# Retention norms: the epsilon row is added to one partition of a square on GpSimd, in place of a third product on TensorE

## The chip, the cores and the metric

The kernel runs on one core of one Trainium2 chip. The metric is the time of one execution on the device in microseconds; lower is better. Engines are named as the profile names them: PE is TensorE (matmuls; PEld its weight loads), DVE is VectorE, ACT is ScalarE, POOL is GpSimd and SP is SyncE, which here only issues transfers. An engine works through its own list of instructions in order; a "q" behind its name (SPq, POOLq) is the side that waits and issues.

## What is computed

A trunk of two layers over x of 1024 positions by 1024 features, in float32. Layer 0 mixes by forgetting attention, layer 1 by retention; each is followed by a SwiGLU block, and each block has an RMS norm ahead of it. The change lies in the norm at the end of the retention, over the 512 features of one head:

```python
def retention(h, w_in, w_out):          # 4 heads, 256 key and 512 value features each
    ...
    _, y = lax.scan(step, state0, (qc, kc, vc))
    y = y.transpose(1, 0, 3, 2, 4).reshape(B, S, H, dv)
    mu = jnp.mean(y, axis=-1, keepdims=True)
    var = jnp.mean(jnp.square(y - mu), axis=-1, keepdims=True)
    y = ((y - mu) * lax.rsqrt(var + EPS)).reshape(B, S, H * dv).astype(h.dtype)
    return (jax.nn.silu(g) * y) @ w_out
```

## The kernel before

Activations are kept transposed: features lie on the 128 partitions, positions along the row, in halves of 512 positions. Float32 products are made of three products in a faster format: each operand is split into a high part (ACT, line 105) and the rest (DVE, line 106), and high x high, high x low and low x high are accumulated in one bank of PSUM. So most work of PE comes as triples of matmuls over 512 columns, each triple waiting for a split by ACT and DVE.

The retention's core runs over eight stages: four heads `h`, and for each the two halves `ib` of the positions. They are called (h, ib) here. The loop at the end of the code below makes, for each stage, the weighted sums over the values (`weighted`, lines 1206 to 1208; four banks of PSUM, one for each 128 of the 512 features), puts the scores of the next stage between them (`scores`, lines 1180 to 1182; their splits at lines 105, 106, 1195, 1196), and ends with `finish`. Ahead of a head's first use, `prepare` loads its keys and queries (`load_parts`, line 1109: eight transfers on POOL's queue for the keys, eight for the queries, each 128 x 512) and its values (SP's queue, line 1095).

`finish` is the norm of a stage. For each of the four groups of 128 features ACT copies the bank to SBUF (line 1227) and squares it (line 1232 for the first group, straight into the sum `yacc`; line 1235 for the others), and DVE adds each further square to `yacc` (line 1236). The sum is split into `ah` and `al`, and PE adds up its 128 partitions with a matrix of ones (lines 1241 and 1243, into the bank `sm`). The values were divided by factors that differ from position to position, so epsilon becomes a row of its own, one number for each position. Before the change that row stands, split into high and low part, in two partitions of a tile `ez` whose other partitions are zero, and a third product with the matrix of ones (line 1242) adds it to the sums. ACT and DVE then make the inverse root (lines 1245 to 1249), and DVE scales the four groups (line 1251; for head 0 also by the gate, line 1255).

The epsilon rows are made once, ahead of the stages: a transposed tile of 32 x 128 is scaled and split (lines 1082 and 1083) and written to DRAM (`ed`, line 1086, POOL's queue). Line 1088 sets the whole of `ez` to zero. Each stage loads its 512 numbers of both rows into `ez` (line 1222, POOL's queue). There is one buffer `ez`, so the load for the next stage waits until line 1242 of this stage has read it.

The order of instructions on each engine isn't that of the code: a scheduler sets it by a model of the times (`schedule_with_timeline_sim=True`), and may also move an instruction that the change doesn't touch. POOL's list holds the loads of line 1109, those of line 1222 and, with the change, the additions; each waits in that order.

Of the kernel before, what the change touches and what calls it, by code (L numbers as in the profile page):

```python
# [10 lines left out]
F32 = mybir.dt.float32  # L11
F32R = mybir.dt.float32r
AF = mybir.ActivationFunctionType
ALU = mybir.AluOpType
# [3 lines left out]
P = 128  # L18
S = 1024
D = 1024  # L20
KT = D // P
H = 512
TB = S // P
EPS = 1e-6
FOX_HEADS = 8
RET_HEADS = 4
# [11 lines left out]
def trunk(ctx, tc, nc, d, out):  # L38
    cp = ctx.enter_context(tc.tile_pool(name="cp", bufs=1))
    yp = ctx.enter_context(tc.tile_pool(name="yp", bufs=16))  # L40
    dp = ctx.enter_context(tc.tile_pool(name="dp", bufs=1, space=DRAM))
# [6 lines left out]
    onesr = cp.tile([P, P], F32R, tag="ones", name="ones")  # L48
# [5 lines left out]
    R = cp.tile([P, S], F32, tag="R", name="R")  # L54
# [4 lines left out]
    def nm(s):  # L59
        cnt[0] += 1  # L60
        return f"{s}_{cnt[0]}"
# [10 lines left out]
    def mm_ps():  # L72
        tag, n = (("mm", 3), ("st", 2), ("pv", 2), ("mm", 3), ("st", 2), ("pv", 2), ("mm", 3))[banks[0] % 7]
        banks[0] += 1
        return mp.tile([P, H], F32, tag=tag, name=nm("mm"), bufs=n)

    def yu(s):
        return yp.tile([P, H], F32, tag="y", name=nm(s))

    def yr(s):  # L80
        return yp.tile([P, H], F32R, tag="y", name=nm(s))
# [22 lines left out]
    def split(hi, lo, src):  # L104
        nc.scalar.copy(hi, src)  # L105
        return nc.vector.tensor_tensor(lo, src, hi.bitcast(F32), op=ALU.subtract)  # L106
# [102 lines left out]
    with ExitStack() as fs:  # L209
# [6 lines left out]
        def half(tag, bufs=2):  # L216
            if tag in ("t", "x"):
                return yp.tile([P, H], F32, tag="y", name=nm(tag))
            return fp.tile([P, H], F32, tag=tag, name=nm(tag), bufs={"rec": 1}.get(tag, bufs))
# [4 lines left out]
        for kt in range(KT):  # L224
            xs = []
            for h in range(2):
                t = half("t", 9)
# [215 lines left out]
        for h in range(2):  # L443
            ks.append([fp.tile([P, S], F32R, tag=t, name=nm(t)) for t in ("kh", "kl")])
            for b in range(2):
                tag, n = (("mm", 3), ("mm", 3), ("st", 2), ("st", 2))[2 * h + b]
# [23 lines left out]
        for h in range(FOX_HEADS):  # L470
            if h > 0:
                kk, qq = k1 if h == 1 else k_head(h), q_head(h)
                if h % 2 == 0:
                    vs, _ = v_pair(h // 2, rc)
# [15 lines left out]
        for i, (n, b) in enumerate(TILES):  # L490
            if i < 3:
                mm_u(ops[n, b], wo[n][6:], last_o[:1], b, first=False, last=(i < EVAC))
            else:
                if n == len(wo):
                    wo.append(wtile(d["fox_o"][n][:, :7 * P], 7))
                tag, bufs = TAGS[i]
# [14 lines left out]
    sp = ctx.enter_context(tc.tile_pool(name="sp", bufs=1))  # L511
# [22 lines left out]
    class Combos:  # L534
# [27 lines left out]
        def finish(self):  # L562
            for n in self.rest[0]:
                for j in range(4):
                    self.t[n][j] = bsplit(self.pools[n], self.rest[j][n])
# [370 lines left out]
    for n in range(KT):  # L936
# [5 lines left out]
        for b in range(2):  # L942
            if (n, b) in ops:
                ps = ops[n, b]
            elif n < NPART:
                ps = mp.tile([P, H], F32, tag=("pv", "st")[b], name=nm("mm"), bufs=2)
            else:
                ps = mm_ps()
# [129 lines left out]
    ps = mp.tile([P, H], F32, tag="ms", name=nm("tr"))  # L1078
    n = RET_HEADS * TB
    nc.tensor.transpose(ps[:n, :P], rho.rearrange("p h b -> p (h b)"), ident)  # L1080
    er = [yr("er")[:n, :P] for _ in range(2)]
    nc.scalar.activation(er[0], ps[:n, :P], AF.Copy, scale=512 * EPS)
    nc.vector.scalar_tensor_tensor(er[1], ps[:n, :P], 512 * EPS, er[0].bitcast(F32), op0=ALU.mult, op1=ALU.subtract)
    ed = dp.tile([2, RET_HEADS * S], F32, tag="ed", name="ed")
    for i, t in enumerate(er):
        nc.gpsimd.dma_start(ed[i].rearrange("(n p) -> n p", p=P), t.bitcast(F32))
    ez = sp.tile([P, H], F32R, tag="xo", name="ez", bufs=2)
    nc.scalar.activation(ez, R[:, :H], AF.Copy, scale=0.0)

    mask = sp.tile([P, H], F32, tag="xo", name="mask", bufs=2)  # L1090
    nc.sync.dma_start(mask, d["ret_mask"])
# [127 lines left out]
                nc.tensor.matmul(yps[vt], sl[:, vs], qh, start=False, stop=False)  # L1219

    def finish(h, ib, yps):
        nc.gpsimd.dma_start(ez.bitcast(F32)[:2, :], ed[:, h * S + ib * H:h * S + (ib + 1) * H])
        acc = sp.tile([P, H], F32, tag="sacc", name=nm("yacc"), bufs=2)
        ys = []
        for vt in range(4):
            y = yu("yt")
            cp_ = nc.scalar.copy(y, yps[vt])
            if vt == h == ib == 0:
                with tc.issue_after(cp_.ins):
                    nc.scalar.preload_act_table_set("natural_log_exp_and_others")  # L1230
            if vt == 0:
                nc.scalar.activation(acc, y, AF.Square)
            else:
                sq = yu("sq")
                nc.scalar.activation(sq, y, AF.Square)
                nc.vector.tensor_tensor(acc, acc, sq, op=ALU.add)
            ys.append(y)
        hi, lo = yr("ah"), yr("al")
        split(hi, lo, acc)
        ps = mp.tile([P, H], F32, tag="ms", name=nm("sm"))  # L1240
        nc.tensor.matmul(ps, onesr, hi, start=True, stop=False)
        nc.tensor.matmul(ps, onesr, ez, start=False, stop=False)
        nc.tensor.matmul(ps, onesr, lo, start=False, stop=True)
        q, fb = yu("q"), yu("fb")
        nc.scalar.activation(q, ps, AF.Ln, scale=1.0 / 512)
        nc.scalar.activation(q, q, AF.Exp, scale=-0.5)
        nc.vector.scalar_tensor_tensor(fb, ps, -0.5 / 512, q, op0=ALU.mult, op1=ALU.mult)
        nc.vector.tensor_tensor(fb, fb, q, op=ALU.mult)
        nc.vector.scalar_tensor_tensor(fb, fb, 1.5, q, op0=ALU.add, op1=ALU.mult)
        for vt in range(4):  # L1250
            nc.vector.tensor_tensor(ys[vt], ys[vt], fb, op=ALU.mult)
            if h < 1:
                g = yu("g")
                nc.sync.dma_start(g, gd[4 * h + vt][:, HALF[ib]])
                nc.vector.tensor_tensor(ys[vt], ys[vt], g, op=ALU.mult)
            nc.sync.dma_start(zd[4 * h + vt][:, HALF[ib]], ys[vt])
# [5 lines left out]
    for i, (h, ib) in enumerate(stages):  # L1262
        nxt = stages[i + 1] if i < 7 else None
        if ib == 1 and nxt:
            prepare(h + 1)
        yps = [mm_ps() for _ in range(4)]
        if ib == 1:
            crossed(h, yps)
        an = []
        for dg in range(4):  # L1270
            if nxt:
                an.append(scores(*nxt, dg))
            weighted(h, ib, dg, a[dg], yps)
        a = an
        finish(h, ib, yps)
        if ib == 1 and nxt:
            heads[h + 1][4] = state(h + 1, heads[h + 1][1], heads[h + 1][3])
# [4 lines left out]
    for n in range(KT):  # L1282
        w = wtile2(d["ret_o"][n], 8)
        for h in range(2):
            ps = mm_ps()
            mm_u(ps, w, acts, h)
            y[n][h] = yu("y")
            xo = sp.tile([P, H], F32, tag="sc", name=nm("xo"), bufs=4)
# [98 lines left out]
```

## Time and profile before

| | us |
|---|---|
| median of three runs | 2575.42 |
| lowest and highest of them | 2571.53, 2575.9 |
| the profiled execution | 2571.2 |
| its span, from the first to the last instruction | 2569.4 |

The profile is of one execution. Its rows give times in us from the start of the span; a row of the timeline is the start, the length, the engine, the line, the operation, the tiles that it writes and reads, their shapes and a count. In brackets stands how long the engine had been idle before, and what ended that. Lines are those of the kernel before (L1242 is line 1242). Matmuls overlap, so their lengths are longer than the step from one start to the next. The eight products of line 1242 start between 1631.6 and 1764.3 us.

### The profile page before, as it was taken

To read this page: it belongs to the slowest core of one execution; us is meant where nothing else is said; L and a number is where in the kernel's file an instruction comes from. 1 tells how busy PE (TensorE), PEld (TensorE's weight loads), DVE (VectorE), ACT (ScalarE), POOL (GpSimd) and SP (SyncE) were. 2 spreads that over 40 slices of the span, in tenths; PEclk is the share of its full clock that TensorE was granted. 3 is DMA by queue.
4 is the path that set the end of the run, shared out by engine and by line. 5 is a ranking of instruction groups with operands and counts; after the bars stand their busy time and mean duration, and the time that the engine had idled before them with its cause. 6 is when DMAs were issued, how large, how long until landed. Compare 5 with 4: busy or idle time off the path is not lost.

```text
span 2569.4 us, 35133 instructions
## 1 busy us (share of the span) xinstructions
PE 2546.4 (99%) x12653; PEld 2165.3 (84%) x12653; DVE 1846.1 (72%) x3093; ACT 1250.2 (49%) x2345; POOL 240.5 (9%) x263
## 2 busy tenths in 40 slices
PE   9999999999999999999999999999999999999998
PEld 8889887888888887889898989888888888888888
DVE  6798888976666777886666566786568666668695
ACT  6566656643333455454344445673354333335543
POOL 0143323000000001001111111210000000000200
PEclk9999999999999999999999999999999999999999
DMA  3111142432332344533343335866522223225541
GB/s 131 46 58 58 58 144 83 159 111 99 111 104 96 120 162 159 176 111 118 109 156 127 124 127 174 280 226 219 193 98 86 107 99 111 103 82 192 170 151 66
DMA packets 145903, 327.92 MB, mean 128 GB/s; under 512 B 17552, under 2 KB 30896, under 8 KB 145728
## 3 DMA queue, kind: packets, MB, share of 16 engines
q1 hardware_dynamic: 136368, 297.79, 33.9%
q0 software_dynamic: 8640, 27.34, 3.1%
q8 instruction: 99, 1.62, 0.3%
q14 instruction: 76, 0.62, 0.1%
q10 hardware_dynamic: 720, 0.55, 0.1%
HBM read 225.44 MB, written 100.17 MB: 127 GB/s over the span
## 4 chain that ended last, share of the span: by engine, by line
PE 93%; DVE 3%; issue 2%; DMA 1%; ACT 1%; POOL 0%; POOLq 0%; DVEq 0%; ACTq 0%
PE mm L676 18%; PE mm L677 18%; PE mm L678 18%; PE mm L113 7%; PE mm L114 7%; PE mm L115 7%; PE mm L796 2%; PE mm L794 2%; PE mm L795 2%; PE mm L282 1%; PE mm L281 1%; PE mm L280 1%; PE mm L1207 1%; PE mm L1208 1%; PE mm L1206 1%
## 5 line engine op out<-in xcount | busy, mean ns | idle before, releaser
L677 PE MATMUL mm<-b,wh 128*128 128x512 f32 x2128 | 827.9, 389 | 1.2 <-DVE b L106 1.2
L676 PE MATMUL mm<-b,wh 128*128 128x512 f32 x2128 | 825.7, 390 | 1.5 <-DVE 22_1856_9302 L736 1.1
L678 PE MATMUL mm<-b,wl 128*128 128x512 f32 x2128 | 824.4, 389 | 0.0
L105 ACT CAST wh<-st 128x512 fp32r<-128x512 f32 (+4 forms) x450 | 276.1, 615 | 497.0 <-PE mm L677 318.6
L676 PEld LDWEIGHTS mm<-b,wh 128*128 128x128 f32 x2128 | 399.5, 188 | 85.4 <-DVE 22_1856_9302 L736 1.5
L678 PEld LDWEIGHTS mm<-b,wl 128*128 128x128 f32 x2128 | 399.5, 188 | 83.7 <-DVE wl L106 0.3
L677 PEld LDWEIGHTS mm<-b,wh 128*128 128x128 f32 x2128 | 399.5, 188 | 83.5 <-DVE b L106 1.6
L106 DVE TENSOR_TENSOR wl<-st,wh 128x512 fp32r<-128x512 f32 (+4 forms) x450 | 309.5, 692 | 181.6 <-ACT wh L105 174.0
L105 ACT CAST wh<-s 128x512 fp32r<-128x512 f32 x252 | 156.5, 622 | 295.0 <-PE mm L677 260.7
L113 PE MATMUL mm<-b,wh 128*128 128x512 f32 x736 | 285.8, 392 | 8.9 <-ACT b L133 4.9
L114 PE MATMUL mm<-b,wh 128*128 128x512 f32 x736 | 286.7, 390 | 0.0
L115 PE MATMUL mm<-b,wl 128*128 128x512 f32 x736 | 286.4, 390 | 0.0
L106 DVE TENSOR_TENSOR wl<-s,wh 128x512 fp32r<-128x512 f32 x252 | 179.9, 716 | 102.3 <-ACT wh L105 98.2
L113 PEld LDWEIGHTS mm<-b,wh 128*128 128x128 f32 x736 | 138.3, 188 | 39.2 <-ACT b L133 5.6
L115 PEld LDWEIGHTS mm<-b,wl 128*128 128x128 f32 x736 | 138.5, 188 | 28.4
L114 PEld LDWEIGHTS mm<-b,wh 128*128 128x128 f32 x736 | 138.5, 188 | 27.6
L795 PE MATMUL mm<-wl,b 128*128 128x256 f32 x448 | 126.4, 283 | 0.0
L794 PE MATMUL mm<-wh,b 128*128 128x256 f32 x448 | 126.2, 283 | 0.0
L796 PE MATMUL mm<-wh,b 128*128 128x256 f32 x448 | 125.9, 283 | 0.0
L524 POOL DMA_DIRECT2D b<-ac_B x24 | 13.3, 555 | 1195.7 <-PE mm L677 1192.9
L628 DVE TENSOR_TENSOR s<-st 128x512 f32<-128x512 f32 x84 | 58.2, 693 | 77.0 <-DMA st<-ffn_in 37.8
L105 ACT CAST b<-st 128x512 fp32r<-128x512 f32 (+1 forms) x136 | 77.9, 606 | 58.0 <-DVE st L832 17.9
(564 smaller groups left out, 4141.0 us busy)
## 6 DMA issues: line engine op xcount, KB each, us to landing
st<-ffn_in SPq DMA_DIRECT2D x88, 512.0 KB, 3.6
st<-ffn_out_pairs SPq DMA_DIRECT2D x32, 512.0 KB, 4.3
ac_T<-t SPq DMA_DIRECT2D x48, 256.0 KB, 2.3
xo<-xd SPq DMA_DIRECT2D x32, 256.0 KB, 2.9
ac_B<-t SPq DMA_DIRECT2D x32, 256.0 KB, 2.5
st<-ac_T SPq DMA_DIRECT2D x16, 512.0 KB, 4.7
b<-ac_T POOLq DMA_DIRECT2D x32, 256.0 KB, 5.7
st<-ret_qk SPq DMA_DIRECT2D x16, 512.0 KB, 4.3
```

The source lines that it names most:

```text
L105: nc.scalar.copy(hi, src)
L106: return nc.vector.tensor_tensor(lo, src, hi.bitcast(F32), op=ALU.subtract)
L113: nc.tensor.matmul(ps, wh, xh, start=(first and k == 0), stop=False, skip_group_check=free)
L114: nc.tensor.matmul(ps, wh, xl, start=False, stop=False, skip_group_check=free)
L115: nc.tensor.matmul(ps, wl, xh, start=False, stop=(last and k == n - 1), skip_group_check=free)
L628: nc.vector.tensor_tensor(self.s1, self.a21, self.a22, op=ALU.add)
L676: nc.tensor.matmul(ps, hi[:, js], th, start=first and j == 0, stop=False, skip_group_check=True)
L677: nc.tensor.matmul(ps, hi[:, js], tl, start=False, stop=False, skip_group_check=True)
L678: nc.tensor.matmul(ps, lo[:, js], th, start=False, stop=(j == 3), skip_group_check=True)
L794: nc.tensor.matmul(o, th[:, tk], hi[:, js], start=f, stop=False, skip_group_check=True)
L795: nc.tensor.matmul(o, th[:, tk], lo[:, js], start=False, stop=False, skip_group_check=True)
L796: nc.tensor.matmul(o, tl[:, tk], hi[:, js], start=False, stop=(j == 3), skip_group_check=True)
```

## The change

One row of epsilon, unsplit, replaces the two rows. It is loaded into one partition, and POOL adds it to partition 0 of the square of the second group of features (`vt == 1`), before DVE adds that square to `yacc`. The product of line 1242 is gone, and so are the second half of the split, the second write to DRAM and the zeroing of `ez`.

```diff
-    er = [yr("er")[:n, :P] for _ in range(2)]
-    nc.scalar.activation(er[0], ps[:n, :P], AF.Copy, scale=512 * EPS)
-    nc.vector.scalar_tensor_tensor(er[1], ps[:n, :P], 512 * EPS, er[0].bitcast(F32), op0=ALU.mult, op1=ALU.subtract)
-    ed = dp.tile([2, RET_HEADS * S], F32, tag="ed", name="ed")
-    for i, t in enumerate(er):
-        nc.gpsimd.dma_start(ed[i].rearrange("(n p) -> n p", p=P), t.bitcast(F32))
-    ez = sp.tile([P, H], F32R, tag="xo", name="ez", bufs=2)
-    nc.scalar.activation(ez, R[:, :H], AF.Copy, scale=0.0)
+    er = yu("er")[:n, :P]
+    nc.scalar.activation(er, ps[:n, :P], AF.Copy, scale=512 * EPS)
+    ed = dp.tile([1, RET_HEADS * S], F32, tag="ed", name="ed")
+    nc.gpsimd.dma_start(ed[0].rearrange("(n p) -> n p", p=P), er)
+    ez = sp.tile([P, H], F32, tag="xo", name="ez", bufs=2)[:1, :]
...
     def finish(h, ib, yps):
-        nc.gpsimd.dma_start(ez.bitcast(F32)[:2, :], ed[:, h * S + ib * H:h * S + (ib + 1) * H])
+        nc.gpsimd.dma_start(ez, ed[:, h * S + ib * H:h * S + (ib + 1) * H])
...
                 nc.scalar.activation(sq, y, AF.Square)
+                if vt == 1:
+                    nc.gpsimd.tensor_tensor(sq[:1, :], sq[:1, :], ez, op=ALU.add)
                 nc.vector.tensor_tensor(acc, acc, sq, op=ALU.add)
...
         nc.tensor.matmul(ps, onesr, hi, start=True, stop=False)
-        nc.tensor.matmul(ps, onesr, ez, start=False, stop=False)
         nc.tensor.matmul(ps, onesr, lo, start=False, stop=True)
```

The scheduler's order changes with it, at many places between the eight stages. Lines after the change are three lower than before up to `finish` (line 1106 is the old 1109, 1177 the old 1180), and line 1234 is the new addition.

On POOL, ahead of stage (1, 0), before: the keys and then the queries of head 1 (`kd1`, `qd1`), and after all of them the epsilon load for stage (0, 1).

```order
L1109 DMA b_15773<-kd11h 128x512
L1109 DMA b_15774<-kd11l 128x512
L1109 DMA b_15803<-qd10h 128x512
L1109 DMA b_15804<-qd10l 128x512
L1109 DMA b_15807<-qd11h 128x512
```

The same place after the change:

```order
L1106 DMA b_15769<-kd11h 128x512
L1106 DMA b_15770<-kd11l 128x512
L1234 TENSOR_TENSOR sq_15709<-sq_15709,ez 1x512
L1219 DMA ez<-ed 1x16x32
L1106 DMA b_15799<-qd10h 128x512
L1106 DMA b_15800<-qd10l 128x512
L1106 DMA b_15803<-qd11h 128x512
```

The addition of stage (0, 0) and the next epsilon load now stand between the keys and the queries of head 1. In the same way the addition of (0, 1) stands ahead of head 2's keys, that of (1, 0) ahead of head 3's keys, and that of (1, 1) ahead of head 3's queries.

On PE, at the sum of stage (0, 0), before (`ah`, `al` are the parts of the sum of squares, `ez` the epsilon rows; the products of line 1180 are the first that read head 1's queries, `b_15803`):

```order
L1207 MATMUL mm_15870<-wl_15632,b_15483 128x384
L1241 MATMUL sm_15730<-ah_15726,ones 128x512
L1242 MATMUL sm_15730<-ez,ones 128x512
L1208 MATMUL mm_15870<-wh_15631,b_15484 128x384
L1206 MATMUL mm_15869<-wh_15658,b_15489 128x256
L1243 MATMUL sm_15730<-al_15727,ones 128x512
L1207 MATMUL mm_15869<-wl_15659,b_15489 128x256
L1208 MATMUL mm_15869<-wh_15658,b_15490 128x256
L1180 MATMUL mm_15895<-b_15803,b_15761 128x512
```

And after:

```order
L1203 MATMUL mm_15865<-wh_15654,b_15485 128x256
L1240 MATMUL sm_15727<-ah_15723,ones 128x512
L1204 MATMUL mm_15865<-wl_15655,b_15485 128x256
L1205 MATMUL mm_15865<-wh_15654,b_15486 128x256
L1241 MATMUL sm_15727<-al_15724,ones 128x512
L1203 MATMUL mm_15866<-wh_15654,b_15485 128x256
L1177 MATMUL mm_15891<-b_15799,b_15757 128x512
```

The product with `ez` is gone, and the sum and its neighbours have changed places by one to three instructions; the first product with head 1's queries (now `b_15799`) follows the same work as before.

On DVE, at the accumulations of stage (0, 0) (line 1236 before, 1235 after), before:

```order
L1138 SCALAR_TENSOR_TENSOR b_15787<-mm_15781,kap_15354,b_15786 128x256
L1236 TENSOR_TENSOR yacc_15706<-yacc_15706,sq_15713 128x512
L1138 SCALAR_TENSOR_TENSOR b_15787<-mm_15781,kap_15354,b_15786 128x256
L1236 TENSOR_TENSOR yacc_15706<-yacc_15706,sq_15718 128x512
L1236 TENSOR_TENSOR yacc_15706<-yacc_15706,sq_15723 128x512
```

And after:

```order
L1135 SCALAR_TENSOR_TENSOR b_15783<-mm_15777,kap_15354,b_15782 128x256 x2
L1235 TENSOR_TENSOR yacc_15702<-yacc_15702,sq_15709 128x512
L1235 TENSOR_TENSOR yacc_15702<-yacc_15702,sq_15715 128x512
L1235 TENSOR_TENSOR yacc_15702<-yacc_15702,sq_15720 128x512
```

The accumulation that waits for POOL has moved one instruction back. SP's list is the same but for a few exchanges; the load of the decay mask (line 1091 before, 1088 after) has moved forward, out of the projections of the retention into the end of layer 0's SwiGLU block.

## The prediction

> **What bounds the kernel now.** I read the page first (busy time by engine, then the chain of work that ended last), then the busy time of each engine in the stretch of the retention that the change touches, then TensorE's waits there. All times are of the profiled execution: 2571.2 us, of which its span is 2569.4 and 1.8 lies around it.
>
> ```profile
> PE 2546.4 (99%) x12653; PEld 2165.3 (84%) x12653; DVE 1846.1 (72%) x3093; ACT 1250.2 (49%) x2345; POOL 240.5 (9%) x263
> ...
> PE 93%; DVE 3%; issue 2%; DMA 1%; ACT 1%; POOL 0%; POOLq 0%; DVEq 0%; ACTq 0%
> ```
>
> Beside each engine stand its busy time in us, the share of the span and the instructions; the second line is the chain. TensorE (PE) is busy for 99% of it and makes 93% of the chain. The other engines are far from it on average, which says little about a single stage.
>
> ```profile
> 1632.00:1655.00 23.00, 23.00 (x136) 20.80 (x135) 20.73 (x47) 14.81 (x34) 5.24 (x10) 1.00 0.73 247
> 1673.00:1690.00 17.00, 17.00 (x95) 15.13 (x93) 15.76 (x35) 12.72 (x29) 5.09 (x10) 1.00 0.82 273
> 1706.00:1725.00 19.00, 19.00 (x107) 17.09 (x106) 17.36 (x37) 14.77 (x33) 1.05 (x2) 1.00 0.31 112
> ```
>
> Each row is a stretch of the retention: its length, then busy us of PE, PEld, DVE, ACT and POOL, the granted clock (1.00 throughout), the share of the DMA engines and GB/s. PE is busy for every microsecond of these three. DVE comes close: it is idle for 2.27 us of 23, 1.24 of 17 and 1.64 of 19.
>
> ```profile
> PE mm L1206 <- DVE atd L1191: 0.2, 1, 0.2
> PE mm L1206 <- ACT wh L1195: 0.2, 1, 0.2
> ```
>
> These are all the waits of PE from 1596 to 1766 us: 0.4 us. So a PE instruction taken out of this stretch is time saved, and anything else counts only if it makes PE wait.
>
> **The change, part by part.** *Eight products go.* Each of the eight stages (four heads, two halves of the positions, called (head, half) below) had one product of the epsilon rows.
>
> ```profile
> L1242 PE MATMUL sm<-ez,ones x8: 389/394/396, 1631.6 to 1764.3; 128*128 128x512 f32 x8
> ...
> 1631.41 0.40 PE L1241 MATMUL sm<-ah,ones 128*128 128x512 f32 x1
> 1631.65 0.39 PE L1242 MATMUL sm<-ez,ones 128*128 128x512 f32 x1
> 1631.88 0.33 PE L1208 MATMUL mm<-wh,b 128*128 128x384 f32 x1
> ```
>
> The products overlap, so what one costs is not its 0.39 us but the time from its start to the next start: 1631.88 - 1631.65 = 0.23 us. Eight of them: 1.84 us, all of it on the path, since PE does not wait there. This term is the gain.
>
> *Small operations that go*: ACT's zeroing of the epsilon tile, one split row on DVE and one of two writes to DRAM. PE did not wait for any of them, so I take nothing; at most it could be the 0.68 us of one full DVE operation (a row below).
>
> *Eight additions on GpSimd come in*, between ACT's square of the second 128 rows and DVE's accumulation of it. In stage (0,0):
>
> ```profile
> 1622.49 0.63 ACT L1235 ACTIVATE sq<-yt 128x512 f32<-128x512 f32 x1
> ...
> 1622.93 0.48 DVE L1138 SCALAR_TENSOR_TENSOR b<-mm,kap,b 128x256 fp32r<-128x256 f32 x1
> 1623.33 0.68 DVE L1236 TENSOR_TENSOR yacc<-yacc,sq 128x512 f32<-128x512 f32 x1
> ```
>
> The square ends at 1622.49 + 0.63 = 1623.12 and DVE takes it at 1623.33; the addition has to come between. DVE is then in an operation whose first input (mm) lies in PSUM. No row shows GpSimd on one partition with 512 elements; the nearest rows are these:
>
> ```profile
> L997 POOL TENSOR_TENSOR m<-m,m x16: 1283/1458/3483, 1154.4 to 1546.5; 128x512 f32<-128x512 f32 x16
> ...
> L365 POOL COPY mx<-t 128x128 f32<-128x128 f32 x8 | 4.0, 498 | 0.3
> ...
> 1538.67 1.29 POOL L997 TENSOR_TENSOR m<-m,m 128x512 f32<-128x512 f32 x1 [21.00 <-DVE m L995]
> 1546.50 3.48 POOL L997 TENSOR_TENSOR m<-m,m 128x512 f32<-128x512 f32 x1 [4.84 <-DMA qd31l<-m]
> ...
> 1539.05 1.46 DVE L106 TENSOR_TENSOR wl<-s,wh 128x512 fp32r<-128x512 f32 x1
> 1540.55 1.66 DVE L651 TENSOR_TENSOR s<-st,s 128x512 f32<-128x512 f32 x1
> 1546.34 0.68 DVE L651 TENSOR_TENSOR s<-st,s 128x512 f32<-128x512 f32 x1
> ```
>
> GpSimd's 128x512 additions took 1.28 to 3.48 us; a copy of a quarter of the elements 0.50. So the addition costs 0.5 to 3.5 us. I take 1.29, the row nearest in kind and length. The last rows show why it spreads. At 1546.50 GpSimd began while DVE ran operation after operation and took 3.48 us. At 1538.67 it took 1.29, and the DVE operations beside it and its successor 1.46 and 1.66, in place of the 0.68 of an undisturbed one (1546.34): up to 0.98 us more. GpSimd and DVE hold each other up, one way or the other.
>
> The Trainium skill speaks against this change: "GPSIMD Engine Reference", section "Engine selection", gives two-input elementwise work to VectorE, since GpSimd is about twice as slow. These rows agree (1.29 against 0.68). By that rule alone eight additions would cost 8 x 1.29 = 10.3 us and the sum would be 8.5 us slower; by the rows PE does not wait for them, and the sum stays a gain. How much of it could reach PE is rival (B).
>
> *What the additions delay on DVE.* DVE works in order, so its accumulation now waits for GpSimd, and what is queued behind it waits too: operand splits for the next stage's products. I looked for the PE products whose operand was ready last before they started.
>
> ```profile
> 1638.60 0.62 ACT L1235 ACTIVATE sq<-yt 128x512 f32<-128x512 f32 x1
> ...
> 1642.67 0.68 DVE L1236 TENSOR_TENSOR yacc<-yacc,sq 128x512 f32<-128x512 f32 x1
> 1645.86 0.48 DVE L1196 SCALAR_TENSOR_TENSOR wl<-mm,kap,wh 128x256 fp32r<-128x256 f32 x1
> ...
> 1647.19 0.34 PE L1207 MATMUL mm<-wl,b 128*128 128x384 f32 x1
> ...
> 1729.59 0.64 ACT L1235 ACTIVATE sq<-yt 128x512 f32<-128x512 f32 x1
> 1740.95 0.61 ACT L105 CAST ah<-yacc 128x512 fp32r<-128x512 f32 x1
> ...
> 1731.75 0.68 DVE L1236 TENSOR_TENSOR yacc<-yacc,sq 128x512 f32<-128x512 f32 x1
> ...
> 1742.69 0.40 PE L1241 MATMUL sm<-ah,ones 128*128 128x512 f32 x1
> ```
>
> In stage (0,1) the square ends at 1639.22 and DVE comes to it at 1642.67, 3.45 us later: the addition is over, and only the 0.98 us of a held operation is left. The tightest split ends at 1645.86 + 0.48 = 1646.34, and its product starts at 1647.19: 0.85 us of cover, so 0.13 us may show. In stage (3,0) there are 1.52 us between square and accumulation, enough for 1.29; the split of the sum ends at 1741.56 and its product starts at 1742.69, 1.13 us of cover against 0.98. Elsewhere the cover is longer. I take 0.3 us for all stages.
>
> *What the additions delay on GpSimd's own queue.* The order of the changed program puts the addition of (0,0) ahead of the eight loads of head 1's queries, with the load of the next epsilon row between them. They had been issued from 1616.08 on.
>
> ```profile
> 1616.08 0.54 POOL L1109 DMA_DIRECT2D b<-qd10h  x1 [2.34 <-PE mm L1208]
> 1618.12 0.54 POOL L1109 DMA_DIRECT2D b<-qd11l  x1 [0.15 <-issue]
> ...
> b<-qd10h POOLq DMA_DIRECT2D x2, 256.0 KB, 5.7
> ...
> b<-qd20h POOLq DMA_DIRECT2D x2, 256.0 KB, 7.6
> b<-qd21l POOLq DMA_DIRECT2D x2, 256.0 KB, 9.3
> ...
> 1632.64 0.69 PE L1180 MATMUL mm<-b,b 128*128 128x512 f32 x3
> 1635.34 0.39 PE L1181 MATMUL mm<-b,b 128*128 128x512 f32 x1
> ```
>
> Now the first of them follows the addition: 1623.12 + 1.29 + 0.54 for one issue = 1625.0 us. With the landing time of head 1's query loads (5.7 us) it lands at 1630.7. The product that needs it (line 1180) starts at 1632.64, or 0.23 earlier without the epsilon product: 1.7 us to spare. The fourth load, 2.04 us behind, is issued at 1627.0, lands at 1632.7 and is needed at 1635.34: 2.4 to spare. So I cost this move at nothing; the cover is thin and is the first rival. Head 2's keys move too, behind the addition of (0,1):
>
> ```profile
> 1632.98 0.56 POOL L1109 DMA_DIRECT2D b<-kd20h  x1
> ...
> 1665.78 0.57 PE L1180 MATMUL mm<-b,b 128*128 128x512 f32 x2
> ```
>
> They had been issued from 1632.98; now the square (1639.22), the addition and an epsilon load come first: 1641.1, 8 us later. The first product of their stage starts at 1665.78, over 20 us behind, so this costs nothing even with a landing of 10 us. The other loads stand behind squares where they stood behind a product of the same stage, which runs later, so they come no later.
>
> *SP's queue*: the load of the decay mask moves forward, between the two loads of the first row below.
>
> ```profile
> 1068.36 2.50 SPq L818 DMA_DIRECT2D st<-ffn_out  x2
> ...
> L1091 SPq DMA_DIRECT2D mask<-ret_mask x1: 422/422/422, 1166.4 to 1166.4; - x1
> ```
>
> The old place is at 1166.4 us. The load is made once, and the view of PE's waits is empty from 1040 to 1180 us: nothing, with that landing of 4.9 us as the most.
>
> **Sum:** -1.84 + 0.3 = -1.5 us, a profiled execution of 2569.7 us. The runs of before lie higher, 2571.53 to 2575.9 with a median of 2575.42, and the profiled one below all of them. Taking 1.5 off both ends (2571.2 and 2575.9) gives 2569.7 to 2574.4. I predict the middle, **2572.0**. A difference under 0.2% (5.15 us) can hardly be told from no change in a measurement of this kernel, so the forecast is "the same".
>
> **Rivals.** *(A) Head 1's queries come late.* It decides if the load chain loses the 1.7 us. With an addition of 3.48 us the first load is issued at 1627.1, and with the landing of head 2's queries (7.6 us) it lands at 1634.7, 2.3 late; the fourth, issued at 1629.2 with 9.3, lands at 1638.5, 3.4 late for its product. PE then waits 3.4 us in this one place: -1.84 + 3.4 = +1.6, a profiled 2572.8. For it: the DMA engines were 73% busy in the stretch from 1632. Against: near 1623 DVE was not in a run like that of 1546.
>
> *(B) DVE becomes the bound: slower.* If in the three dense stretches each addition waits as long as the longest row (3.48) with DVE standing behind it, and holds one DVE operation up by 0.98 more, DVE loses 3 x 4.46 = 13.4 us; its idle time there is 5.15 and the cover at the tightest product 0.85, so PE waits about 7.4 us: +5.6, a profiled 2576.8. PE starts to wait at 2.0 us of loss per addition ((5.15 + 0.85) / 3), and the gain is used up at 2.6. For it: the rows of 1546 and the shares above. Against: DVE reaches most of these accumulations over a microsecond after the square, and two dense stretches have no tight product. The skill's page "SBUF — State Buffer", section "SBUF: two separate sides", tells of a port pair that either a GpSimd operation or a VectorE operation with two SBUF inputs holds to its end while the other waits. By that page an addition gets in at the next DVE operation that reads PSUM, which these stages have after every few, so the page makes the long wait less likely; the rows of 1538 and 1546 agree with it.
>
> *(C) The change doesn't do what it says*: the scheduler has reordered products around the removed ones, and PE ends as late as before, 2571.2. Against: 0.4 us of waits, so less work must end earlier.
>
> A larger gain has no place to come from: with the 0.4 us of waits gone too, 2568.9.
>
> **How the numbers follow.** Forecast 0.64; (A) 0.13; (B) 0.10; (C) 0.08; 0.05 that runs which scatter by 4.4 us show over 0.2% faster without a cause in the program. Only (B) is slower by over 0.2%: 0.10. Faster 0.05. Same 0.64 + 0.13 + 0.08 = 0.85. The range goes from just under the lowest gain, 2568.0, to the slow end of the timed runs with (A) and about half of (B), 2579.0.
>
> **What would show it.** PE's instructions in this stretch end 1.5 us earlier and its waits stay under 1 us: right. The addition's row: 1.3 us on average for 1x512, with some longer. A wait of line 1177 (the old 1180) for a load of the queries near 1632 would be (A). Waits of PE for split operands or for the sum's product, with DVE waiting for the addition's line, would be (B). I am wrong if GpSimd needs over 3 us for most additions, or if an addition between loads costs more than its own time.

## The result, and the profile after

| | before | after |
|---|---|---|
| median of 21 runs each, us | 2572.3 | 2578.98 |
| lowest and highest, us | 2570.09, 2575.9 | 2575.34, 2582.66 |
| ratio after to before, 95% interval | | 1.0025 (1.0019 to 1.0031) |
| the profiled execution, us | 2571.2 | 2579.58 |

The changed kernel is 0.25% slower, some 6.5 us, where 1.5 us less had been forecast.

Busy time by engine and the chain of work that ended last, of the kernel after:

```profile
PE 2550.7 (99%) x12645; PEld 2167.2 (84%) x12645; DVE 1852.5 (72%) x3092; ACT 1249.6 (48%) x2344; POOL 251.0 (10%) x270
PE 93%; DVE 3%; issue 2%; ACT 1%; DMA 1%; POOL 0%; DVEq 0%; POOLq 0%; ACTq 0%
```

The averages look as before: PE 99%, DVE 72%, ACT 48 in place of 49%, POOL 10.5 us more. They don't show the loss. Next, the start of one product just ahead of the eight stages and of one just behind them, before:

```profile
1590.54 0.40 PE L676 MATMUL mm<-b,wh 128*128 128x512 f32 x1
...
1769.97 0.39 PE L114 MATMUL mm<-b,wh 128*128 128x512 f32 x1
```

and the same two products after:

```profile
1591.19 0.40 PE L676 MATMUL mm<-b,wh 128*128 128x512 f32 x1
...
1778.90 0.39 PE L114 MATMUL mm<-b,wh 128*128 128x512 f32 x1
```

From one to the other it took 1769.97 - 1590.54 = 179.43 us before and 1778.90 - 1591.19 = 187.71 after: **8.28 us more in the eight stages**, although eight products of 0.23 us are gone there. The rest of the program takes almost the same time, 0.65 us more ahead of the stages and about 0.5 less behind them. The same difference is the column "in the stages" of the table of experiments below.

The three stretches that the prediction called dense, after (length, busy us of PE, PEld, DVE, ACT and POOL, clock, DMA share, GB/s):

```profile
1632.00:1655.00 23.00, 23.00 (x135) 20.88 (x134) 20.99 (x41) 14.65 (x34) 10.11 (x18) 1.00 0.90 309
1673.00:1690.00 17.00, 15.65 (x87) 13.82 (x86) 14.11 (x28) 10.69 (x24) 3.63 (x6) 1.00 0.57 183
1706.00:1725.00 19.00, 17.73 (x90) 14.77 (x89) 18.01 (x34) 12.39 (x28) 4.14 (x4) 1.00 0.39 139
```

PE, which had been busy throughout, is idle for 1.35 us of the second stretch and 1.27 of the third. In the second, DVE is not busier but less: it is idle for 17 - 14.11 = 2.9 us, where it had been 1.24. So PE waits there while DVE has time to spare, and it is not DVE's amount of work that binds. In the third, DVE is the busier one (idle 0.99 us, 1.64 before), and this view alone can't tell its amount of work from its order there.

What PE waited for between 1596 and 1766 us (total, times, longest):

```profile
PE sm L1240 <- ACT ah L105: 2.4, 2, 2.3
PE mm L1149 <- DVE wl L1193: 1.4, 1, 1.4
PE mm L1177 <- DVE wl L1193: 0.8, 1, 0.8
PE mm L1203 <- ACT wh L1192: 0.8, 1, 0.8
PE mm L1214 <- DVE atd L1188: 0.8, 1, 0.8
PE sm L1241 <- DVE al L106: 0.3, 1, 0.3
```

6.5 us in all, against 0.4 before: seven waits, of products of six lines. Each is released by work of DVE or ACT on scores or sums, none by GpSimd. The additions themselves, with shortest, median and longest in ns:

```profile
L1234 POOL TENSOR_TENSOR sq<-sq,ez x8: 1278/1284/1828, 1624.2 to 1762.0; 1x512 f32<-1x512 f32 x8
```

That is the 1.29 us that had been assumed. Beside six of the eight, a DVE operation with two inputs in SBUF took 0.8 to 1.1 us longer. Two DVE rows of line 832, the first beside the addition of 1735.13, the second undisturbed:

```profile
1735.50 2.00 DVE L832 TENSOR_TENSOR st<-st,st 128x1024 f32<-128x1024 f32 x1 [0.28 <-DMA st<-gd]
1740.73 1.22 DVE L832 TENSOR_TENSOR st<-st,st 128x1024 f32<-128x1024 f32 x1 [0.57 <-DMA st<-gd]
```

But no wait of DVE for line 1234 is in its view. The loss has another way, and stage (1,0) shows it. After, in rows of ACT, POOL, DVE and PE:

```profile
1663.90 0.68 ACT L1232 ACTIVATE sq<-yt 128x512 f32<-128x512 f32 x1
1670.17 0.73 ACT L1095 ACTIVATE b<-st,vmean 128x512 fp32r<-128x512 f32 x1 [5.58 <-PE mm L1204]
...
1661.93 1.77 POOL L1234 TENSOR_TENSOR sq<-sq,ez 1x512 f32<-1x512 f32 x1 [6.54 <-DMA st<-vd]
...
1670.93 0.75 DVE L1096 SCALAR_TENSOR_TENSOR b<-st,vmean,b 128x512 fp32r<-128x512 f32 x1 [3.46 <-ACT b L1095]
1671.60 0.69 DVE L1235 TENSOR_TENSOR yacc<-yacc,sq 128x512 f32<-128x512 f32 x1
1674.44 0.61 DVE L1193 SCALAR_TENSOR_TENSOR wl<-mm,kap,wh 128x384 fp32r<-128x384 f32 x1
1675.56 0.68 DVE L1235 TENSOR_TENSOR yacc<-yacc,sq 128x512 f32<-128x512 f32 x1
...
1675.20 0.47 PE L1149 MATMUL mm<-b,b 128*128 128x512 f32 x1 [1.35 <-DVE wl L1193]
```

The last square of the stage ended at 1663.90 + 0.68 = 1664.58 and the addition at 1661.93 + 1.77 = 1663.70. From then on the inputs of all three accumulations (line 1235) were ready. But on DVE stands ahead of them a split of the next head's values (line 1096), which waits for ACT's half of it (line 1095), and ACT, by its release, for a product of PE (line 1204). So DVE sat idle for 3.46 us with the accumulations behind it, and then made them among the splits of the scores: 1671.60, 1673.38, 1675.56. PE waited 1.35 us for the row of line 1193 at 1674.44. Before, DVE's list had it the other way round:

```profile
1667.72 1.48 DVE L1236 TENSOR_TENSOR yacc<-yacc,sq 128x512 f32<-128x512 f32 x2
1670.76 0.74 DVE L1099 SCALAR_TENSOR_TENSOR b<-st,vmean,b 128x512 fp32r<-128x512 f32 x1
```

The accumulations came first (the last two from 1667.72), the value split at 1670.76. Counted among the instructions that both kernels have, the DVE list of after has the three accumulations and the split of the sum 6, 4, 9 and 14 places later in this stage, and 11, 12, 14 and 15 later in (1,1).

In stage (3,0) PE waits for ACT:

```profile
1745.89 0.63 ACT L105 CAST wh<-st 128x512 fp32r<-128x512 f32 x1 [2.56 <-DMA st<-ret_o]
1748.28 0.62 ACT L105 CAST wh<-st 128x512 fp32r<-128x512 f32 x1 [1.76 <-DMA st<-ret_o]
1749.34 0.62 ACT L105 CAST ah<-yacc 128x512 fp32r<-128x512 f32 x1
...
1750.01 0.50 PE L1240 MATMUL sm<-ah,ones 128*128 128x512 f32 x1 [2.25 <-ACT ah L105]
```

The split of the sum (`ah`) stands behind two splits of weights for the output projection, which are still being loaded. PE waits 2.25 us. Before, the two splits stood ahead of `ah` as well, but their loads came in time:

```profile
1739.24 1.29 ACT L105 CAST wh<-st 128x512 fp32r<-128x512 f32 x2 [0.77 <-DMA st<-ret_o]
```

Then `ah` followed at 1740.95. So here it is not ACT's order at this place that is new but the time of the loads: SP issued the two at 1733.59 and 1735.40 before, and at 1741.98 and 1744.59 after. What held them back was followed one step only: SP's waits just ahead of them are ended above all by DVE's work on the gates and splits (lines 832 and 106), and SP's own list differs a little too. After the wait the granted clock fell to one half for a while (a window, then the first product in it and the first behind it):

```profile
1752.00:1754.00 2.00, 2.00 (x6) 1.51 (x6) 1.43 (x3) 1.12 (x2) 0.00 (x0) 0.50 0.89 285
...
1751.37 0.63 PE L115 MATMUL mm<-b,wl 128*128 128x512 f32 x1
1754.78 0.39 PE L114 MATMUL mm<-b,wh 128*128 128x512 f32 x1
```

From 1751.37 to 1754.78 eight products took 3.41 us, 0.43 each in place of 0.23: another 1.6 us. Waits (6.5 - 0.4 = 6.1), the clock (1.6) and the products that are gone (-1.84) make 5.9 of the 8.28 us. The rest was not taken apart; a part of it are longer steps right behind the waits (0.56 and 0.33 us behind the product of 1750.01, in place of 0.23).

### The profile page after: what moved, and what is told of

Read it like the earlier page. It is cut to its first block, busy times and chain, and to the rows that moved or that the text cites. A ratio compares the mean times of both kernels' runs of the same rounds, so it can differ in the third digit from the quotient of the medians.

```text
span 2577.8 us, 35135 instructions
## 1 busy us (share of the span) xinstructions
PE 2550.7 (99%) x12645; PEld 2167.2 (84%) x12645; DVE 1852.5 (72%) x3092; ACT 1249.6 (48%) x2344; POOL 251.0 (10%) x270
## 4 chain that ended last, share of the span: by engine, by line
PE 93%; DVE 3%; issue 2%; ACT 1%; DMA 1%; POOL 0%; DVEq 0%; POOLq 0%; ACTq 0%
PE mm L676 19%; PE mm L677 19%; PE mm L678 19%; PE mm L113 7%; PE mm L115 7%; PE mm L114 7%; PE mm L796 2%; PE mm L794 2%; PE mm L795 2%; PE mm L280 1%; PE mm L282 1%; PE mm L281 1%; PE mm L1203 1%; PE mm L1204 1%; PE mm L1205 1%
```

## The experiments

Theories. *Hold*: GpSimd's additions hold DVE operations up, and the delay adds up along DVE until PE waits. *Order*: in the scheduler's new order DVE's and ACT's work for the next products comes behind operations that wait; the additions as such cost little. *Wait*: DVE waits for GpSimd.

The fourteen variants were timed in five rounds against the kernel before, whose median was 2572.4 to 2573.5 us beside them.

| run | what | median us | ratio (95% interval) | in the stages, us | waits of PE, us |
|---|---|---|---|---|---|
| after | the change | 2578.98 | 1.0025 (1.0019 to 1.0031) | +8.3 | 6.5 |
| e1_none | no additions | 2582.41 | 1.0032 (1.0020 to 1.0045) | +10.4 | 9.4 |
| e2_unused | additions that nobody reads | 2575.07 | 1.0006 (0.9997 to 1.0015) | +2.3 | 3.5 |
| e3_32cols | additions of 32 columns | 2580.14 | 1.0025 (1.0015 to 1.0036) | +6.8 | 5.6 |
| e4_vector | additions on VectorE | 2574.70 | 1.0006 (0.9997 to 1.0015) | +1.3 | 2.9 |
| e5_order_before | the change, PE, DVE, ACT in the old order | 2571.53 | 0.9995 (0.9986 to 1.0004) | -0.9 | 1.2 |
| e6_order_after | the work of before, in the new order | 2577.89 | 1.0023 (1.0014 to 1.0032) | +6.4 | 5.0 |
| e7_none_order_before | no epsilon at all, old order | 2579.64 | 1.0026 (1.0015 to 1.0036) | +7.6 | 5.8 |
| e8_none_own_order | no epsilon at all, own order | 2579.24 | 1.0027 (1.0016 to 1.0038) | +3.8 | 5.0 |
| e9_32cols_order_before | 32 columns, old order | 2571.94 | 0.9990 (0.9981 to 0.9998) | -1.8 | 0.6 |
| e10_dve_act_order_before | the change, DVE and ACT in the old order | 2571.75 | 0.9991 (0.9982 to 0.9999) | -0.8 | 1.0 |
| e11_pe_order_before | the change, PE in the old order | 2579.02 | 1.0020 (1.0011 to 1.0029) | +8.1 | 7.2 |
| e12_vector_order_before | additions on VectorE, old order | 2572.50 | 0.9994 (0.9984 to 1.0003) | -0.1 | 1.6 |
| e13_dve_order_before | the change, DVE in the old order | 2574.64 | 1.0008 (0.9999 to 1.0017) | +1.4 | 2.4 |
| e14_act_order_before | the change, ACT in the old order | 2577.22 | 1.0017 (1.0009 to 1.0026) | +3.6 | 4.3 |

The last two columns are from the profiled execution, the waits from 1590 to 1780 us. They are of one execution each: that of e9 was the fastest of its eleven (2568.26 us), that of e14 too (2574.73). Half clock lies in the stages in after, e1, e3, e7 and e11 alone, for 3.41 to 10.24 us, and adds to their loss there.

### Four variants of the addition

e1_none:

```diff
-                if vt == 1:
-                    nc.gpsimd.tensor_tensor(sq[:1, :], sq[:1, :], ez, op=ALU.add)
```

> The changed kernel without the additions: the epsilon row is loaded but never added (epsilon is left out), the eight products stay gone. VectorE's order of the accumulations is that of the kernel before, within a few instructions. All theories: 1.8 us faster than the kernel before (2570.5 against 2572.3), TensorE's waits from 1590 to 1780 us under 1 us. If it is not faster, the removal of the product itself costs something through the order on TensorE, and neither hold nor wait is the cause.

It was the slowest of all. One wait of PE carries most of it:

```profile
PE mm L1177 <- DMA b<-qd10h: 7.1, 1, 7.1
```

Head 1's queries came 7.1 us late. With no addition to wait for, the epsilon loads of seven stages ran one after the other on GpSimd's queue, each for the landing of the one before, and the query loads stood behind them. As a control it was worthless, but it is the first rival of the prediction in the flesh.

e2_unused:

```diff
-                    nc.gpsimd.tensor_tensor(sq[:1, :], sq[:1, :], ez, op=ALU.add)
+                    sx = yu("sx")
+                    nc.gpsimd.tensor_tensor(sx[:1, :], sq[:1, :], ez, op=ALU.add)
```

> GpSimd makes the same additions but writes them to a tile that nobody reads (epsilon is left out), so VectorE never depends on GpSimd, and the order of the accumulations is near that of the kernel before. Hold theory (each addition holds up one VectorE operation with two inputs in SBUF by about 1.0 us, 6 of 8 in the changed kernel, 6.1 us in all, and VectorE has no idle time to make it up in stages (1,0) to (3,0)): 2 to 6 us slower than the kernel without additions, with operations of 1.7 us on VectorE beside the additions. Order theory and wait theory: as fast as the kernel without additions, 1.8 us under the kernel before.

Between the two: 2.3 us lost in the stages, with the additions present and nobody waiting for them. Its order is a third one, so this alone decides nothing.

e3_32cols:

```diff
-                    nc.gpsimd.tensor_tensor(sq[:1, :], sq[:1, :], ez, op=ALU.add)
+                    nc.gpsimd.tensor_tensor(sq[:1, :32], sq[:1, :32], ez[:, :32], op=ALU.add)
```

> The addition on GpSimd covers 32 of the 512 columns (epsilon is left out of the other 480). The dependency square, GpSimd, VectorE stays, and the order of VectorE's accumulations in stages (1,0) and (1,1) is as late as in the changed kernel (71, 73, 77, 85 and 111, 114, 119, 122 instructions behind the first, against 66, 72, 73, 74 and 97, 101, 104, 107 before). Hold theory: the hold shrinks with the operation, so no more than 1 us of waits is left and the time is 1 to 2 us under the kernel before. Order theory: as slow as the changed kernel, 5 to 7 us over the kernel before.

The longest of its waits, at a place of the changed kernel:

```profile
PE mm L1149 <- DVE wl L1193: 2.0, 1, 2.0
```

The additions are all but gone (0.24 us in the median, in place of 1.28), their dependency and the late accumulations are there, and the ratio is that of the changed kernel, 1.0025. This speaks against the hold theory: with hardly a hold left, nothing is won.

e4_vector:

```diff
-                    nc.gpsimd.tensor_tensor(sq[:1, :], sq[:1, :], ez, op=ALU.add)
+                    nc.vector.tensor_tensor(sq[:1, :], sq[:1, :], ez, op=ALU.add)
```

> VectorE itself makes the eight additions of 1x512; nothing is left out. GpSimd only issues loads. If VectorE's time is the bound in these stages (hold theory, in its wider form), eight operations of about 0.6 us, 4.8 us in all, cost nearly as much as the 6.1 us of holds: 2 to 5 us slower than the kernel before. If it takes GpSimd for the loss (wait or hand-over between engines), it is 1.8 us faster than the kernel before.

Neither: about 1.5 us slower, and unclear against no change. It has an order of its own as well.

### Holding the order

The four variants differ in order besides what they were meant to differ in. From here on the order was held: for the instructions of the eight stages, edges from each to its predecessor in the other kernel's list of that engine, which set the order of issue and wait for nothing else. `PIN` holds those lists, as instruction numbers, for each engine held. SP's list is held in none of these runs.

```diff
+def _pinned(tc, nc):
+    traced = {i.name: i for i in nc.cur_bb.bb.instructions}
+    for seq in PIN:
+        ...
+        for a, b in zip(v, v[1:]):
+            tc.add_manual_dep(traced["I-%d" % b], "I-%d" % a, mybir.DependencyInfo(
+                mybir.DependencyClass.NoSync, mybir.DependencyReason.DATA), reason="pinned")
...
     with tile.TileContext(nc, schedule_with_timeline_sim=True) as tc:
         trunk(tc, nc, d, out)
+        _pinned(tc, nc)
```

e5_order_before (`PIN`: PE, DVE and ACT of the kernel before, for the instructions of the changed kernel):

> The work of the changed kernel, additions on GpSimd and all, but TensorE, VectorE and ScalarE are held to the order that the kernel before has in the eight stages (edges between neighbours in each engine's list; 3 of 12593 products stand elsewhere, none on VectorE and ScalarE; in the changed kernel it was 169, 71 and 44). Order theory (the loss comes from the new order of the three engines, in which VectorE's work for the next products comes too late): 0 to 2 us faster than the kernel before, waits of TensorE from 1590 to 1780 us of 2 us at most. Hold theory: the holds of about 1 us are still there, so 4 to 7 us slower than the kernel before.

```profile
PE mm L115 <- DVE wl L106: 0.6, 1, 0.6
PE mm L1203 <- ACT wh L1192: 0.6, 1, 0.6
```

The waits are down to 1.2 us and the time is 0.9995 of before. The additions took 1.28 to 3.52 us in this run, longer than in the changed kernel, and DVE waited for them five times, 5.1 us in all. PE hardly noticed, so the wait theory falls with the hold theory.

e6_order_after (`PIN`: PE, DVE and ACT of the changed kernel, for the instructions of the kernel before; each product with `ez` behind the one with `ah`):

> The counterpart: the work of the kernel before, with the eight products and without any addition, but TensorE, VectorE and ScalarE are held to the order of the changed kernel in the eight stages (174, 71 and 44 instructions displaced); GpSimd's queue keeps the order of before. Order theory: 5 to 9 us slower than the kernel before, and TensorE waits at places of the changed kernel (line 1149's, 1177's and 1240's counterparts). Hold theory: as fast as the kernel before within 1 us.

Four of its waits, and a row of DVE (line numbers are those of before):

```profile
PE mm L1152 <- DVE wl L1196: 1.4, 1, 1.4
PE sm L1241 <- ACT ah L105: 1.1, 1, 1.1
PE mm L1180 <- DVE wl L1196: 0.8, 1, 0.8
PE mm L1217 <- DVE atd L1191: 0.8, 1, 0.8
...
1670.60 0.75 DVE L1099 SCALAR_TENSOR_TENSOR b<-st,vmean,b 128x512 fp32r<-128x512 f32 x1 [3.45 <-ACT b L1098]
```

Old lines 1152, 1241, 1180 and 1217 are the new 1149, 1240, 1177 and 1214: the same places, with no addition in the program, and 6.4 us lost in the stages. On DVE the value split before the accumulations of (1,0) waits 3.45 us for ACT, as in the changed kernel (3.46). Three of the waits have the length of the changed kernel's (1.4, 0.8 and 0.8 us, at the new lines 1149, 1177 and 1214). The two runs together show it: **the order makes the loss; in the old order the additions don't.**

Two things stay open. The changed kernel loses more than this run: 8.28 us, and the 1.84 that it should have gained, against 6.4. Its wait for `ah` is 2.25 us long in place of 1.08 and is followed by 1.6 us of half clock, which this run doesn't have; whether the additions have a part in that isn't shown. And SP's list went along with the others: in the stages it is, but for one load, that of before in e5, and that of after in e6. It doesn't make the loss alone, since e11 and e14 below have that of before too, but for one load, and are slow; what it adds isn't separated.

e7_none_order_before and e8_none_own_order (no addition, no epsilon load; the first with `PIN` of PE, DVE and ACT of before):

```diff
-        nc.gpsimd.dma_start(ez, ed[:, h * S + ib * H:h * S + (ib + 1) * H])
...
-                if vt == 1:
-                    nc.gpsimd.tensor_tensor(sq[:1, :], sq[:1, :], ez, op=ALU.add)
```

> Neither products nor additions nor loads of the epsilon rows (epsilon is left out), the three engines held to the order of before. All theories: the eight products alone, 1.8 us faster than the kernel before. It mends the first experiment, in which the loads of the epsilon row, with nobody reading it, all ran ahead of head 1's queries.

> The same work as the run before it (no products, no additions, no epsilon loads; epsilon is left out), in the order that the scheduler itself finds (85 products, 42 operations of VectorE and 21 of ScalarE displaced against before). Order theory: 2 to 6 us slower than the run before it although nothing is computed in addition. Hold theory and a queue theory (a late load): as fast as the run before it, 1.8 us under the kernel before.

Both missed: both runs were slow, and the second no slower than the first. In the first, DVE's waits for the gate rows, PE's waits, and the first load of head 2's queries:

```profile
DVE yt L1250 <- DMA g<-gd: 4.9, 4, 2.6
...
PE mm L1203 <- DVE wl L1193: 3.9, 1, 3.9
PE mm L1203 <- ACT wh L1192: 1.9, 1, 1.9
...
1641.48 0.54 POOL L1106 DMA_DIRECT2D b<-qd20h  x1 [4.07 <-PE mm L1179]
```

The same load before:

```profile
1655.11 0.56 POOL L1109 DMA_DIRECT2D b<-qd20h  x1
```

Before, an epsilon load stood ahead of head 2's queries and waited for the sum of stage (0,1); the queries behind it started at 1655.11. Without it they started at 1641.48: a transfer of two rows of 512 numbers had been holding back eight of 256 KB. DVE waited 4.9 us for the gate rows (`g`), against 2.5 before, and PE 3.9. That the query loads crowd the gate rows on the DMA engines is not shown: the gate loads were also issued later (the first at 1636.8, before at 1633.5), and the first, on which DVE waited longest (2.6 us), had been under way for 4.7 us when the first query load started. PE's other wait came earlier, at 1610.39, behind one of ACT for values that were still being loaded. Around the ends of the two waits the clock stood at one half, for 6.83 and 3.41 us. The second run has 3.2 us of waits for gate rows and so says nothing about the order.

e9_32cols_order_before (e3's edit, `PIN` as in e5):

> The addition on 32 of 512 columns (epsilon left out of the other 480), TensorE, VectorE and ScalarE held to the order of before; GpSimd's queue as in the run of the changed work in that order. If the run without epsilon loads was slow because head 2's query loads, no longer behind a waiting epsilon load, ran into the gate rows that VectorE waits for: this one is 1 to 2.5 us faster than the kernel before, VectorE waits for gate rows under 2 us in all (4.9 there). If the order of before itself has become bad without the products: 4 to 8 us slower again. Against the run with full additions in this order the difference is the price of the holds there: 0 to 1.2 us.

1.8 us won in the stages, the size of the eight products, and no wait of DVE for a gate row in the profile. That it fits to the tenth is luck, since the execution was the fastest of eleven; the ratio alone says 2.6 us, with an interval from 0.5 to 4.9. So the order of before had not made e7 slow. What e7 lacks is the work on GpSimd's queue that holds head 2's loads back: here its keys start at 1639.37 (e7 1632.84) and its queries at 1646.18. Full additions in this order (e5) lie within 1.3 us of it: 0.9995 against 0.9990, with intervals that overlap, and 0.9 us in the stages. So GpSimd's holds and waits cost about 1 us here by the profiled executions, which the timing can't tell from nothing.

### Which engine's order

`PIN` as in e5, for DVE and ACT alone (e10), PE alone (e11), DVE alone (e13), ACT alone (e14); e12 is e4's edit with the `PIN` of e5.

> The changed work with VectorE and ScalarE held to the order of before; TensorE and GpSimd in the scheduler's order (79 products displaced). If it is the order of the splits and accumulations that makes TensorE wait: 0 to 2 us faster than the kernel before. If it is the order of the products themselves: 3 to 7 us slower.

> The changed work with TensorE alone held to the order of before; VectorE, ScalarE and GpSimd in the scheduler's order (36 and 15 displaced on the first two). If the order of the products decides: 0 to 2 us faster than the kernel before. If the order of the splits and accumulations decides: 3 to 7 us slower.

With DVE and ACT held, the accumulations of (1,0) on DVE, and all waits of PE:

```profile
1666.10 0.69 DVE L1235 TENSOR_TENSOR yacc<-yacc,sq 128x512 f32<-128x512 f32 x1 [1.18 <-POOL sq L1234]
1669.50 1.48 DVE L1235 TENSOR_TENSOR yacc<-yacc,sq 128x512 f32<-128x512 f32 x2
1672.60 0.74 DVE L1096 SCALAR_TENSOR_TENSOR b<-st,vmean,b 128x512 fp32r<-128x512 f32 x1
...
PE mm L115 <- DVE wl L106: 0.7, 1, 0.7
PE mm L1203 <- DVE atd L1188: 0.3, 1, 0.3
```

They are back ahead of the value split (1672.60). DVE even waits 1.18 us for GpSimd at the first, and PE doesn't notice. Of the kernels that compute all of the reference it has the lowest ratio, 0.9 in a thousand under before, with an interval that just leaves out no change and overlaps that of e5. With PE held instead, one wait makes most of the loss, and ACT shows why:

```profile
PE sm L1240 <- ACT ah L105: 6.8, 1, 6.8
...
1747.86 0.62 ACT L105 CAST wh<-st 128x512 fp32r<-128x512 f32 x1 [4.11 <-DMA st<-ret_o]
1748.38 0.61 ACT L105 CAST ah<-yacc 128x512 fp32r<-128x512 f32 x1
```

`ah` stood behind three weight splits, one more than before, and the third waited 4.11 us for its load. From 1747.41 the clock stood at one half for 6.83 us.

> The changed work with VectorE alone held to the order of before (TensorE 86 and ScalarE 30 displaced). If the late place of the accumulations in VectorE's list is enough to explain the loss: 0 to 2 us faster than the kernel before. If ScalarE's list (splits of the sum behind splits of weights that are still being loaded) is needed as well: 2 to 6 us slower, with TensorE waiting for ScalarE's part of the sum (line 1240).

> The changed work with ScalarE alone held to the order of before (TensorE 102 and VectorE 44 displaced). If VectorE's list decides: 3 to 7 us slower than the kernel before. If ScalarE's list decides: 0 to 2 us faster.

The ratio goes from 1.0025 to 1.0008 with DVE's old order, to 1.0017 with ACT's, to 0.9991 with both. DVE's alone takes a clear part of the loss away. ACT's part is not clear of the scatter (1.0009 to 1.0026 against 1.0019 to 1.0031), nor is it certain that DVE's is the larger, and in each of the two runs the lists that were not held are new ones too.

> VectorE makes the additions, right before the accumulation that reads them; nothing left out; the three engines held to the order of before. Eight operations of 0.6 us, 4.8 us of VectorE, against holds of about 1 us each by GpSimd: within 1 us of the run with GpSimd's additions in this order, so 0 to 2 us faster than the kernel before. If the extra work on VectorE reaches TensorE: 2 to 4 us slower.

0.9994: in the same order it makes no measurable difference whether GpSimd or VectorE adds, though VectorE's eight additions took 0.67 us each.

## Why the prediction was wrong

- **The products** (-1.84 us): in size nothing speaks against it. e9 gains 1.83 us in the stages, to the tenth by luck; by its ratio 0.5 to 4.9.
- **The small operations and the mask load** (0): nothing in the traces speaks against it.
- **The addition's length** (1.29 us, bounds 0.5 to 3.5): right; 1.28 in the median, 3.52 the longest in e5.
- **What the additions delay on DVE** (0.3 us): this is the step that failed. "I looked for the PE products whose operand was ready last before they started", and "Elsewhere the cover is longer": the cover was read from the trace of before, where DVE and ACT stood in the old order. The changed program has another one, and in it the tightest places are elsewhere. The new lists lay open, but the section on the change shows that of DVE for stage (0,0) alone, where one accumulation had moved back by one; in (1,0) they moved by 4 to 9. In the old order the step was nearly right: e5 and e10 lose 0.9 to 1.0 us against the full gain. The new order alone costs 6.4 us in the stages (e6).
- **GpSimd's queue** (0, first rival at +1.6): right for this kernel. The first of head 1's queries was issued at 1626.48 and landed at 1630.38, against 1625.0 and 1630.7 foreseen, and PE did not wait for any of them. e1 shows what the rival would have looked like.
- **Rival (B), DVE becomes the bound**: right in sign and, by luck, near in time (2576.8 against 2579.58), wrong in the cause. The holds came as described, up to 1.1 us, but shrinking them (e3) won nothing, and in stage (1,0) DVE was idle with its inputs ready. The Trainium skill's page "SBUF — State Buffer", section "SBUF: two separate sides", tells of a port pair held for a whole instruction by GpSimd or by a VectorE operation with two SBUF inputs; the rows agree (2.00 against 1.22 us beside an addition).
- **Rival (C), the scheduler has reordered around the products**: nearest to the mechanism, but it had been priced at no change (2571.2), and it speaks of PE's products. With those back in the old order the loss stayed (e11, 8.1 us); with DVE and ACT in theirs it went (e10). The argument against (C), "less work must end earlier", is what the case refutes: less work in a worse order ended later.

What stays open: why the scheduler chose this order. It had moved accumulations later in kernels with GpSimd's full and short additions alike, so the addition's length alone is not the reason. Which single exchange costs most was not separated either; there are seven waits.

## What to carry to other kernels

Where a scheduler sets the order, a change of one instruction is a change of all lists, and cover that was read from the old trace holds only for the old order: walk the new lists, and look for ready work that has been put behind an operation that waits for a load or a buffer. To learn what an edit itself costs, hold the order of the other engines fixed and time it there. And a small transfer at the head of a queue can be what holds back the large ones behind it.

## What had not been expected of the hardware

The same wait can cost more in one execution than in another. Ahead of the window 438 to 440 us PE waits for the same operation in both kernels, 1.87 us before and 1.84 after. The window before:

```profile
438.00:440.00 2.00, 2.00 (x9) 1.45 (x9) 1.53 (x3) 1.78 (x4) 0.00 (x0) 1.00 0.59 159
```

and after:

```profile
438.00:440.00 2.00, 2.00 (x6) 1.56 (x5) 0.69 (x1) 1.23 (x3) 0.00 (x0) 0.50 0.44 129
```

The granted clock is 1.00 in one and 0.50 in the other, and six products fall into the window in place of nine. The change does not touch this place. The lag of the changed kernel grew from 0.2 to 1.7 us there, which is part of the scatter of single runs. The Trainium skill's page "TensorE: Matmul & The Clock Gate", section "What's actually happening", tells of a clock that goes to one half after an idle window of about 3.4 us, a window that runs freely. The half clock here lasted 3.41 us at 1751.37, which agrees with the window's length. But the waits ahead of it were 2.25 us there and 1.84 at 437 us, less than a window, so by these rows a shorter wait can already bring it on, and needn't.

The clock records of the 16 traces show more. The half clock of one execution starts on a grid of such windows: in the changed kernel at 437.216 and 1751.347, which is 385 times 3.4133 us apart. Cut into windows of this grid, the executions (from 10 to 2550 us) have 19 windows at full clock in which PE was busy for at most 1.6 us, and half clock followed on 17 of them; it followed on 2 of the 11867 others, with 1.60 and 1.87 us. So what counted was how much of a wait fell into one window: at 437 us PE was still busy for 1.57 us of its window after the change, and for 1.65 before.
